# The first quarter of a feed-forward product, all of it in seven block products

## The chip, the cores and the metric

The kernel runs on one core of a Trainium2 chip. The core has five engines with an instruction stream each: TensorE (PE in the profile, its weight loads PEld), VectorE (DVE), ScalarE (ACT), GpSimd (POOL) and SyncE (SP), which here only issues DMAs. An engine works its stream in order, and engines wait for each other through semaphores. PE writes its results into PSUM, from where ACT and DVE take them. The metric is the time of one execution on the device in microseconds, the median of several runs.

## The reference

One layer of a streaming encoder on 512 rows of width 1024, in float32. Three branches of attention are gated, added up and projected; then comes the part that the change touches:

```python
h = h + merged @ w_out[l]
u2 = rmsnorm(h, g_ffn[l])
h = h + jnp.square(jax.nn.relu(u2 @ w_ff1[l])) @ w_ff2[l]
return rmsnorm(h, g_final)
```

`w_ff1` is 1024 x 4096, `w_ff2` 4096 x 1024.

## The kernel before, in words

**Products in three passes.** Operands are split into a high part in a rounded format (`hi`, a cast on ACT) and the remainder (`lo`, a subtraction on DVE). A product is then three matmuls: high by high, high by low, low by high. Every weight chunk of 128 x 1024 numbers (512 KB) is loaded into a buffer `raw`, cast, and subtracted. `raw`, `hi` and `lo` have three buffers each in the pool of weights, so a load waits until the chunk three before it has been split. In the last part every fourth `raw` has a buffer of its own in another pool.

**Seven products for eight.** The feed-forward part runs in four quarters of 1024 hidden columns. A quarter has two halves (`i` = 0, 1). Each half is `u2` (as two by two blocks) times a two by two block of `w_ff1`, computed by a scheme of seven block products (numbered 1 to 7) instead of eight. Products 1, 2 and 3 take a plain weight block ("11", "21", "22"); products 5, 6, 7 and 4 take the sums T1 to T4 of weight blocks. The sums are made in DRAM by DMAs on POOL's queue, early in the program: `sum_ops` lists them, and `next_sum` issues one behind the cast of each weight chunk, at line 131 if it adds to what is there and at 133 if it copies. On the side of the activations product 1, 2, 3 and 4 take a block of `u2`, products 5, 6 and 7 a difference of blocks (`u2s`, high and low part `u2sh`, `u2sl`); one block is replaced by the sum or difference `R7`. A block product is 24 matmuls of 128 x 128 by 256 columns into one PSUM bank; `first_evac` adds the seven up in SBUF, squares the positive part, and splits the result (`ch`, `cl`) for the second product.

**The first quarter is special.** Its second half (`first_product(0, 1)`) runs in block products. Its first half runs as four plain column tiles: tiles 0 and 1 in halves of 256 columns (`half`), between the transposes of the norm, and tiles 2 and 3 (`plain_tile`) as matmuls of 512 columns. So the differences of activations (`u2_sums`, line 1264) are made while the plain tiles run.

**What stands ahead.** The projection by `w_out` runs in two halves of 512 columns; the second one finishes row block by row block (`res_evac`). A finished block is squared and summed on ACT, one small power on POOL gives the norm's factor (`rr`, line 986), DVE scales the block (`un`, line 1190), PE transposes it (`u2_turn`, line 1214), ACT and DVE split it into `u2`, and ACT copies it to `b11` or `b12` (line 1217), from which the differences are made.

**What sets the order.** PE's stream is in the order of the code. The streams of the other engines are put in order by a scheduler from a model of its own; `tc.issue_after(x)` adds that an instruction comes behind `x`.

Of the kernel before, what the change touches and what calls it, by code (L numbers as in the profile page):

```python
# [32 lines left out]
def chunk_list():  # L33
# [24 lines left out]
    L += [("T", "w_ff1", P * j) for j in range(4)]  # L58
    for q in range(4):
        L += [(kind, q, i, b) for kind in "FB" for b in ("11", "21", "12", "22") for i in range(2) if kind == "B" or q or i]  # L60
# [4 lines left out]
def hybrid_block(ctx, tc, chunks, wst, memT, xN, gffn, gfin, wup, cst, out):  # L65
# [45 lines left out]
    tsum = {(n, q): dram.tile([2 if q else 1, P, 1024], F32, name=f"T{n}_{q}") for q in range(4) for n in (1, 2, 3, 4)}  # L111

    def sum_ops():
        for q in range(4):
            for n, src, add in ((1, "11", 0), (3, "12", 0), (1, "12", 1), (3, "22", 1), (2, 1, 0), (2, "22", 1), (4, 2, 0),
                                (4, "21", 1)):
                i = index["F", q, 0 if q else 1, src] if isinstance(src, str) else None
                yield tsum[n, q], tsum[src, q] if i is None else wst[i:i + (2 if q else 1)], add

    sums = sum_ops()  # L120
    chunk_n, cast_now, low_now, hold = [0], [None], [None], [None]

    def next_sum(after):
# [3 lines left out]
        op = next(sums, None) if n > 11 else None  # L127
        if op is not None:
            to, src, add_ = op
            if add_:  # L130
                d = nc.gpsimd.dma_start(to, src, accum_op=ALU.add, max_dma_last_dim=8192)
            else:
                d = nc.gpsimd.dma_start(to, src)
# [857 lines left out]
    with pool("outp") as op_:  # L991
# [28 lines left out]
        def gate_group(gate, wo, oh, ol, i, ready=None, last=None):  # L1020
# [65 lines left out]
            def merge(j):  # L1086
                th = X[j % 4 // 2][:, j % 2, :]
                nc.vector.scalar_tensor_tensor(th, th, 1.0, ys[j], op0=ALU.add, op1=ALU.mult)
                nc.gpsimd.tensor_tensor(acc[j], acc[j], th, op=ALU.add)
# [76 lines left out]
        gate_group("gate_gla", "w_gla_o", ogh, ogl, 1, last=(mh, ml))  # L1166
        hN = [h_tile(t, "h") for t in range(NT)]
# [12 lines left out]
        def res_evac(c):  # L1180
            def go(t, ps):
                cs = slice(512 * c, 512 * c + 512)
                nc.vector.tensor_tensor(hN[t][:, cs], hN[t][:, cs], ps, op=ALU.add)
                sumsq(unp.tile([P, 512], F32, tag="hsq", name=nm("hsq"), bufs=2), hN[t], t, c, c)
                if c == 1:
                    r = rms_tile(unp, t)
                    un[t] = unp.tile([P, D], F32, tag="un", name=nm("un"), bufs=2)
                    for g in range(2):
                        gs_ = slice(512 * g, 512 * g + 512)
                        nc.vector.scalar_tensor_tensor(un[t][:, gs_], hN[t][:, gs_], r, gf[:, gs_], op0=ALU.mult, op1=ALU.mult)  # L1190
            return go

        un = {}
# [14 lines left out]
        ws = [[t.rearrange("p (k c) -> p k c", k=KT) for t in own_w(("T", "w_ff1", P * j))] for j in range(2)]  # L1208

        def u2_turn(t):  # L1210
            for g in range(2):
# [4 lines left out]
                last = split(*(x[:, 2 * g + t // 2, :, sl] for x in u2), pt)  # L1216
# [3 lines left out]
        first = [mmt() for _ in ws]  # L1220

        def half(j, i, ks=range(KT)):
            sl = slice(256 * i, 256 * i + 256)
# [26 lines left out]
    with pool("ff") as yp:  # L1250
# [119 lines left out]
        def first_product(q, i):  # L1370
            for n in FIRST:
# [11 lines left out]
                if q == 0 and n == 2:  # L1383
                    u2_last()
# [222 lines left out]
```

## Time and profile before

| | us |
|---|---|
| median of 3 runs | 816.33 (816.24 to 818.31) |
| profiled execution, its own time | 815.97 |
| its span from the first to the last instruction | 814.2 |
| last merge on POOL ends | 447.5 |
| first and last transposes of the norm begin on PE | 481.10, 493.51 |
| second product begins on PE | 532.63 |

The page of the profile gives busy times by engine, the chain of waits that ended last, and groups of instructions. A row of instructions in order of time has the start in us from the begin of the span, the length in us, engine, line and operation, result and sources (buffer numbers left out), shape, and in brackets the idle time ahead with what ended it. Neighbours on PE overlap, so their distance is what one costs.

### The profile page before, as it was taken

How to read it: one execution, taken by the hardware profiler on the slowest of the kernel's cores; microseconds unless marked ns; L12 is line 12 of the kernel's file. 1: busy time of each engine (PE TensorE's matmuls, PEld its weight loads, DVE VectorE, ACT ScalarE, POOL GpSimd, SP SyncE). 2: the span in 40 equal slices, each digit the busy share in tenths (PEclk: the TensorE clock that was granted, in tenths of full speed). 3: DMA queues.
4: the chain of work that ended last, by engine and by line, in shares of the span. 5: the costliest groups of instructions: out<-in, count | busy, mean ns of one | idle time of the engine just before them, and what ended most of it. 6: DMA issues, size and time to landing. Idle time of an engine off the chain costs nothing.

```text
span 814.2 us, 12430 instructions
## 1 busy us (share of the span) xinstructions
PE 805.0 (99%) x4788; PEld 707.4 (87%) x4788; DVE 590.2 (72%) x913; ACT 438.7 (54%) x694; POOL 103.9 (13%) x127
## 2 busy tenths in 40 slices
PE   9999999999999999999999999999999999999996
PEld 7788888888888888999999889988998899889984
DVE  6857877546455587877567548896788778887896
ACT  7755655443344234444454536774676367637764
POOL 0000110011101212143143000011001100100011
PEclk9999999999999999999999999999999999999999
DMA  9433666688788867757755505878658855895543
GB/s 358 172 116 131 204 165 201 188 240 246 204 250 264 230 215 190 178 151 207 205 131 159 203 1 179 261 160 216 244 165 198 218 216 166 196 253 195 156 84 124
DMA packets 38604, 155.53 MB, mean 191 GB/s; under 512 B 4560, under 2 KB 5008, under 8 KB 36496
## 3 DMA queue, kind: packets, MB, share of 16 engines
q1 hardware_dynamic: 27424, 95.98, 32.8%
q0 software_dynamic: 9328, 54.01, 31.4%
q10 hardware_dynamic: 1792, 4.75, 1.6%
q8 instruction: 37, 0.61, 0.3%
q14 instruction: 23, 0.19, 0.1%
HBM read 152.58 MB, written 31.49 MB: 226 GB/s over the span
## 4 chain that ended last, share of the span: by engine, by line
PE 96%; DVE 1%; issue 1%; DMA 0%; ACT 0%; POOL 0%; POOLq 0%; DVEq 0%; ACTq 0%
PE mm L157 24%; PE mm L158 24%; PE mm L159 24%; PE a L157 5%; PE a L158 5%; PE a L159 5%; PE mm L380 1%; PE a L394 1%; PE a L624 1%; PE a L662 1%; PE a L661 1%; DVE h L1267 1%; PE a L900 1%; PE a L408 1%; DMA mem_s<-in_memT_dram 0%
## 5 line engine op out<-in xcount | busy, mean ns | idle before, releaser
L148 DVE TENSOR_TENSOR wlo<-raw,whi 128x1024 fp32r<-128x1024 f32 x67 | 86.4, 1293 | 58.9 <-ACT whi L147 58.7
L157 PE MATMUL mm<-uhi,whi 128*128 128x512 f32 (+1 forms) x352 | 125.9, 358 | 0.0
L159 PE MATMUL mm<-uhi,wlo 128*128 128x512 f32 (+1 forms) x352 | 123.7, 351 | 0.0
L158 PE MATMUL mm<-ulo,whi 128*128 128x512 f32 (+1 forms) x352 | 123.6, 351 | 0.0
L147 ACT CAST whi<-raw 128x1024 fp32r<-128x1024 f32 x67 | 70.4, 1051 | 92.9 <-PE mm L158 56.0
L1271 ACT CAST hi<-raw 128x1024 fp32r<-128x1024 f32 x65 | 68.2, 1049 | 49.7 <-PE mm L158 32.7
L1273 DVE TENSOR_TENSOR lo<-raw,hi 128x1024 fp32r<-128x1024 f32 x65 | 79.5, 1224 | 17.6 <-ACT hi L1271 17.6
L157 PEld LDWEIGHTS mm<-uhi,whi 128*128 128x128 f32 x352 | 66.7, 189 | 9.9 <-issue 1.5
L159 PEld LDWEIGHTS mm<-uhi,wlo 128*128 128x128 f32 x352 | 66.6, 189 | 9.1
L158 PEld LDWEIGHTS mm<-ulo,whi 128*128 128x128 f32 x352 | 66.7, 189 | 8.1
L1271 ACT CAST hi<-b 128x1024 fp32r<-128x1024 f32 x40 | 41.9, 1048 | 42.0 <-PE mm L159 25.6
L158 PE MATMUL mm<-u2l,hi 128*128 128x256 f32 x224 | 63.4, 283 | 0.0
L159 PE MATMUL mm<-u2h,lo 128*128 128x256 f32 x224 | 63.4, 283 | 0.0
L157 PE MATMUL mm<-u2h,hi 128*128 128x256 f32 x224 | 63.4, 283 | 0.0
L1457 POOL DMA_DIRECT2D b<-in_wst_dram x32 | 27.3, 853 | 271.3 <-DVE lo L1273 208.1
L1273 DVE TENSOR_TENSOR lo<-b,hi 128x1024 fp32r<-128x1024 f32 x40 | 48.9, 1224 | 14.1 <-ACT hi L1271 14.0
L158 PE MATMUL mm<-lo,ch 128*128 128x512 f32 x136 | 52.9, 389 | 0.0
L157 PE MATMUL mm<-hi,ch 128*128 128x512 f32 x136 | 52.9, 389 | 0.0
L159 PE MATMUL mm<-hi,cl 128*128 128x512 f32 x136 | 52.9, 389 | 0.0
L158 PE MATMUL mm<-u2sl,hi 128*128 128x256 f32 x168 | 47.5, 283 | 0.0
L157 PE MATMUL mm<-u2sh,hi 128*128 128x256 f32 x168 | 47.5, 283 | 0.0
L159 PE MATMUL mm<-u2sh,lo 128*128 128x256 f32 x168 | 47.5, 283 | 0.0
(414 smaller groups left out, 2093.2 us busy)
## 6 DMA issues: line engine op xcount, KB each, us to landing
raw<-in_wst_dram SPq DMA_DIRECT2D x114, 512.0 KB
b<-in_wst_dram POOLq DMA_DIRECT2D x32, 512.0 KB, 5.3
raw<-T SPq DMA_DIRECT2D x28, 512.0 KB
T<-in_wst_dram POOLq DMA_DIRECT2D x12, 1024.0 KB, 9.3
b<-in_wst_dram SPq DMA_DIRECT2D x16, 512.0 KB
wb<-in_wst_dram POOLq DMA_DIRECT2D x15, 512.0 KB, 5.3
wb<-in_wst_dram SPq DMA_DIRECT2D x8, 512.0 KB
nFb<-dF ACTq DMA_DIRECT2D x6, 512.0 KB
```

Of the source, the lines that this page charges most:

```text
L147: cast = nc.scalar.copy(hi, raw)
L148: low_now[0] = nc.vector.tensor_tensor(lo, raw, f(hi), op=ALU.subtract).ins
L157: nc.tensor.matmul(ps, lh, rh, start=start, stop=False, skip_group_check=on)
L158: nc.tensor.matmul(ps, lh, rl, start=False, stop=False, skip_group_check=on)
L159: nc.tensor.matmul(ps, ll, rh, start=False, stop=stop, skip_group_check=on)
L380: nc.tensor.matmul(kps[h], w[:, h * P:(h + 1) * P], x[:, k, :], start=k == p == 0, stop=k == KT - 1 and p == 2)
L394: nc.tensor.matmul(ps, x[:, k, sl], w[low][:, kk, :], start=k == low == 0 and x is mxh, stop=k == KT - 1 and low == 1)
L408: nc.tensor.transpose(pt[:, t * P:(t + 1) * P], xn[:, t, k * P:(k + 1) * P], ident)
L624: nc.tensor.matmul(ps[e], q[a, sl], k[a, :w], start=p == 0, stop=p == 2)
L1271: nc.scalar.copy(hi, raw)
L1273: nc.vector.tensor_tensor(lo, raw, f(hi), op=ALU.subtract)
L1457: nc.gpsimd.dma_start(to[i], wst[index["B", q, i, x]], accum_op=ALU.add)
```

## The change

The four plain tiles are gone; half 0 of the first quarter runs in block products too, with its own chunks of `w_ff1` (loads of "F" chunks instead of "T" chunks). The halves take turns: product 1 and 2 of half 0, then of half 1, then 5, 5, 6, 6, 3, 3, 7, 7, 4, 4. Each half has two PSUM banks, and some products are added up there: 6, 7 and 4 are accumulated onto 1, and 3 onto 5. For that the sign of product 6's difference is turned round. A product of this list runs its high-weight passes first and the low-weight ones last (`low_last`). The evacuations, casts, subtractions and loads of this quarter are written out in one list, and `in_order` keeps that order on DVE, ACT and SP. Eight more sums (a fifth group of T1 to T4, for half 0) are issued on POOL's queue two at a time behind the casts of `w_out` chunks, after the last merge. The load of the last norm's gains (`gl`) is put behind the loads of the last quarter's blocks.

POOL's stream between the last merge and the norm, before (`acc`: merges; `rr`: powers of the norm; waits in brackets are semaphores of the engines and of DMA landings):

```order
L1089 TENSOR_TENSOR acc6_1905<-acc6_1905,ct_630_4085 128x512 [waits DVE_49,Pool_49]
L1089 TENSOR_TENSOR acc7_1906<-acc7_1906,ct_630_4085 128x512 [waits DVE_49,Pool_49]
L1089 TENSOR_TENSOR acc4_1903<-acc4_1903,ct_629_4084 128x512 [waits DVE_49,Pool_49]
L1089 TENSOR_TENSOR acc5_1904<-acc5_1904,ct_629_4084 128x512 [waits DVE_49,Pool_49]
L986 TENSOR_TENSOR rr_706_4614<-ms_705_4613,mhalf_73 128x1 [waits DVE_49]
L986 TENSOR_TENSOR rr_710_4648<-ms_709_4647,mhalf_73 128x1 [waits DVE_49]
```

and after:

```order
L1089 TENSOR_TENSOR acc5_1908<-acc5_1908,ct_629_4088 128x512 [waits DVE_49,Pool_49]
L133 DMA T1_4_93<-in_wst_dram 16x8192 [waits DMASW7_49]
L133 DMA T3_4_95<-in_wst_dram 16x8192
L131 DMA T1_4_93<-in_wst_dram 64x2048 [waits DMASW7_49]
L131 DMA T3_4_95<-in_wst_dram 64x2048 [waits DMASW2_49,DMASW0_49]
L133 DMA T2_4_94<-T1_4_93 16x8192 [waits DMASW3_49,DMASW1_49,Activation_49]
L131 DMA T2_4_94<-in_wst_dram 64x2048 [waits DMASW3_49]
L133 DMA T4_4_96<-T2_4_94 16x8192 [waits DMASW4_49,Activation_49]
L131 DMA T4_4_96<-in_wst_dram 64x2048 [waits DMASW6_49,DMASW5_49]
L986 TENSOR_TENSOR rr_706_4626<-ms_705_4625,mhalf_73 128x1 [waits DVE_49]
L986 TENSOR_TENSOR rr_710_4660<-ms_709_4659,mhalf_73 128x1 [waits DVE_49]
```

Eight DMAs now stand ahead of the first power, six of which wait for the landing of an earlier one of the eight.

DVE's stream from the last differences on, before (`b`: differences of activations; `u2sl` their low parts; `lo` low parts of weights; `R`: the half-wide sums):

```order
L1264 TENSOR_TENSOR R70_4912<-b111_4415,b110_4414 128x512
L211 TENSOR_TENSOR u2sl_4915<-b121_4417,u2sh_4914 128x1024
L1264 TENSOR_TENSOR R71_4913<-b111_4415,b110_4414 128x512
L211 TENSOR_TENSOR u2sl_4915<-b120_4416,u2sh_4914 128x1024
L211 TENSOR_TENSOR u2sl_4915<-b110_4414,u2sh_4914 128x1024
L1273 TENSOR_TENSOR lo_754_5050<-raw_752_5047,hi_753_5049 128x1024
```

and after, from the second difference's low part on:

```order
L1357 TENSOR_TENSOR lo_750_4982<-raw_745_4892,hi_749_4981 128x1024
L1367 TENSOR_TENSOR u2sl_4877<-b110_4418,u2sh_4876 128x1024
L1283 TENSOR_TENSOR ev1_4865<-ev1_4865,mm_724_4714 128x512
L1357 TENSOR_TENSOR lo_753_5016<-raw_748_4950,hi_752_5015 128x1024
L1280 TENSOR_TENSOR R70_4874<-b111_4419,b110_4418 128x512
L1280 TENSOR_TENSOR R71_4875<-b111_4419,b110_4418 128x512
```

Between the differences stand now the low parts of the weights of products 5 and 6 and the additions of products 1 and 2.

ACT's stream after, where product 6 of half 1 gets its weights (`hi_755`; `raw_751` holds them):

```order
L1365 CAST u2sh_4876<-b110_4418 128x1024
L1353 CAST hi_752_5015<-raw_748_4950 128x1024
L1413 COPY od0_4866<-mm_723_4713 128x512
L1305 ACTIVATE ev1_4865<-ev1_4865 128x512
L1306 ACTIVATE ev1_4865<-ev1_4865 128x512
L1365 CAST u2h_4406<-R70_4874 128x512
L1365 CAST u2h_4406<-R71_4875 128x512
L1353 CAST hi_755_5053<-raw_751_4988 128x1024
```

The cast of these weights stands behind the casts of both `R`; before, the casts of `R` stood among the plain tiles' evacuations.

The diff, cut to its core:

```diff
-    L += [("T", "w_ff1", P * j) for j in range(4)]
...
-    tsum = {(n, q): dram.tile([2 if q else 1, P, 1024], F32, name=f"T{n}_{q}") for q in range(4) for n in (1, 2, 3, 4)}
+    tsum = {(n, q): dram.tile([2 if 0 < q < 4 else 1, P, 1024], F32, name=f"T{n}_{q}") for q in range(5) for n in (1, 2, 3, 4)}
...
+    sums, late_sums = islice(sum_ops(), 32), islice(sum_ops(), 32, None)
...
+        for to, src, add_ in islice(late_sums if late_on else sums, 1 + len(late_on)):
+            with tc.issue_after(merged[0]) if late_on else ExitStack():
+                if add_:
+                    d = nc.gpsimd.dma_start(to, src, accum_op=ALU.add, max_dma_last_dim=8192)
+                else:
+                    d = nc.gpsimd.dma_start(to, src)
...
-        ws = [[t.rearrange("p (k c) -> p k c", k=KT) for t in own_w(("T", "w_ff1", P * j))] for j in range(2)]
+        ws = [own_w(("F", 0, 0, b)) for b in ("11", "21")]
...
-                last = split(*(x[:, 2 * g + t // 2, :, sl] for x in u2), pt)
+                if g or t < 2:
+                    last = split(*(x[:, 2 * g + t // 2, :, sl] for x in u2), pt)
...
+            for low in range(1 + low_last):
+                for a in range(2):
+                    for k in range(4):
+                        if not low:
+                            mm(a, k, wh, uh, k == 0 if go is None else go and a == k == 0, False)
+                            mm(a, k, wh, ul, False, False)
+                        if low or not low_last:
+                            mm(a, k, wl, uh, False, k == 3 and (go is None or a == 1))
+                        yield
...
         u2_turn(2)
-        half(0, 0)
-        half(1, 0, range(4))
+        run(first_mms(1, ws[0], banks[0][0], True))
+        rest = first_mms(2, ws[1], banks[0][1], True)
+        run(islice(rest, 4))
         norm_end = u2_turn(3)
-        half(1, 0, range(4, KT))
-        half(0, 1)
-        half(1, 1)
+        run(rest)
...
+            for n, behind in ((1, added[3]), (2, scaled[3])):
+                get(n, 1)
+                high(n, 1)
+                with tc.issue_after(behind):
+                    low(n, 1)
+            get(5, 0)
+            get(5, 1)
+            mms(1, 1)
+            mms(2, 1)
+            with tc.issue_after(norm_end), in_order():
+                nc.scalar.copy(o11[0], flat[0][1])
+                sub(b_22, b_21, b_22)
+                high(5, 0)
+                add(o11[0], flat[0][0])
+                part(sums[0], b_22)
+                low(5, 0)
+                get(6, 0)
+                part(sums[0], b_22, True)
+                mms(5, 0)
+                relu2(o11[0])
+                sub(b_21, b_11, b_21)
+                sub(b_11, b_22, b_11)
+                high(5, 1)
+                nc.scalar.copy(o11[1], flat[1][1])
+                left_high(0, 0, o11[0])
+                part(sums[1], b_11)
+                low(5, 1)
+                get(6, 1)
+                mms(5, 1)
+                part(sums[1], b_11, True)
+                high(6, 0)
+                add(o11[1], flat[1][0])
+                low(6, 0)
+                get(3, 0)
+                mms(6, 0)
+                nc.scalar.copy(o22[0], flat[0][1])
+                relu2(o11[1])
+                for k in range(2):
+                    sub(R7[k], b_12[:, 512 * k:512 * k + 512], b_11[:, 512 * k:512 * k + 512], ALU.add)
+                    part(fours[k], R7[k])
+                high(6, 1)
+                for k in range(2):
+                    part(fours[k], R7[k], True)
+                low(6, 1)
+                get(3, 1)
+                mms(6, 1)
...
-        plain_evac(0, first[0])
-        plain_evac(1, first[1])
-        plain_tile(2)
-        u2_sums()
-        plain_tile(3)
-        load_blocks(0)
-        first_product(0, 1)
+        first_quarter()
         second_product(0)
```

`high` is the cast of a weight chunk, `low` its subtraction, `get` its load, `part` the high or low part of a difference, `mms` the 24 matmuls of one product; the rest of the list goes on in the same way through products 3, 7 and 4.

More of the change, by code (lines that the diff above doesn't have):

```diff
@@ L1 @@
-from contextlib import ExitStack
+from contextlib import ExitStack, contextmanager
 from functools import partial
@@ L126, in next_sum @@
         n = chunk_n[0]
[L127 to L133, printed above, removed]
+        if n <= 11:
+            return
+        for to, src, add_ in islice(late_sums if late_on else sums, 1 + len(late_on)):
[4 more added lines that the diff above has]
+                    d = nc.gpsimd.dma_start(to, src)
             tc.add_manual_dep(d.ins, after.name, mybir.DependencyInfo(mybir.DependencyClass.Sync, mybir.DependencyReason.DATA),
```

196 lines of the change are left out of this document (127 added, 69 removed).

## The prediction

> **What bounds the kernel now.** I read the page's busy shares and its chain first, then the instructions in order of time around the place of the change.
>
> ```profile
> PE 805.0 (99%) x4788; PEld 707.4 (87%) x4788; DVE 590.2 (72%) x913; ACT 438.7 (54%) x694; POOL 103.9 (13%) x127
> PE 96%; DVE 1%; issue 1%; DMA 0%; ACT 0%; POOL 0%; POOLq 0%; DVEq 0%; ACTq 0%
> ```
>
> TensorE (PE) carries 96% of the chain that ends last, so a product that is left out is worth its issue interval, as long as its operands come in time. The next rows (instructions on PE in order of time: start, length, line, operation) mark the stage.
>
> ```profile
> 481.10 1.03 PE L1214 MATMUL a<-cst_s,un 128*128 128x128 f32 x8
> ...
> 493.51 1.04 PE L1214 MATMUL a<-cst_s,un 128*128 128x128 f32 x8
> 494.30 0.36 PE L157 MATMUL mm<-u2h,f3h 128*128 128x256 f32 x1
> ...
> 501.57 0.40 PE L157 MATMUL mm<-u2h,whi 128*128 128x512 f32 x1
> ...
> 512.48 0.28 PE L157 MATMUL mm<-u2h,hi 128*128 128x256 f32 x1
> ...
> 532.63 0.40 PE L157 MATMUL a<-hi,ch 128*128 128x512 f32 x1
> ```
>
> 481.10 is the first transpose of the normed rows (row block 0), 493.51 the last (block 3). From 494.30 stand 60 matmuls of 256 columns (rest of tiles 0 and 1), from 501.57 48 of 512 (tiles 2 and 3), from 512.48 168 of 256 (the seven block products of half 1); at 532.63 the second product begins. That is 7.27/60 = 0.121, 10.91/48 = 0.227 and 20.15/168 = 0.120 us each. Lengths of 0.28 and 0.40 overlap; only the distances count. There is no hole in this stage to win back.
>
> **The change, part by part.** *Products on PE.* In the first half of the quarter four column tiles (96 matmuls of 256 and 48 of 512) give way to 168 of 256. Up to 494.30 nothing moves: 36 matmuls of the first products stand before the last transposes in both. After it come 12 + 12 x 24 = 300 matmuls of 256, at 0.120 us 36.0 us, where 38.33 (532.63 - 494.30) stood: **-2.36 us** if every operand is there. The 512-wide matmul costs 0.227, less than two halves (0.240), so leaving out an eighth of the block work saves only 6% of the stage.
>
> *First wait: the first block product with a summed operand.* Product 5 of half 0 needs a difference of activations that only the last transposes complete. Before, 18 us of plain tiles covered it; now 12 + 48 matmuls, until 494.30 + 60 x 0.120 = 501.5. The costs, from before's ScalarE (ACT) and VectorE (DVE) rows:
>
> ```profile
> 495.49 1.18 ACT L1217 COPY b<-a 128x512 f32<-128x512 f32 x2 [0.27 <-DVE u2l L211]
> 502.27 1.04 ACT L210 CAST u2sh<-b 128x1024 fp32r<-128x1024 f32 x1
> 507.01 1.05 ACT L1271 CAST hi<-raw 128x1024 fp32r<-128x1024 f32 x1 [0.77 <-PE mm L158]
> 508.60 0.62 ACT L210 CAST u2h<-R 128x512 fp32r<-128x512 f32 x1
> 516.39 0.58 ACT L1347 COPY ev<-mm 128x512 f32<-128x512 f32 x1
> ...
> 495.97 2.35 DVE L148 TENSOR_TENSOR wlo<-raw,whi 128x1024 fp32r<-128x1024 f32 x2
> 499.37 3.74 DVE L1264 TENSOR_TENSOR b<-b,b 128x1024 f32<-128x1024 f32 x3
> 503.76 1.22 DVE L211 TENSOR_TENSOR u2sl<-b,u2sh 128x1024 fp32r<-128x1024 f32 x1
> 518.43 0.69 DVE L1349 TENSOR_TENSOR ev<-ev,mm 128x512 f32<-128x512 f32 x1
> ```
>
> The fixed order puts on ACT, ahead of the copy of the last transposed block, the copy of product 2's bank, which waits for product 2: 494.30 + 12 x 0.120 + 0.28 = 496.0. Then ACT does copy 0.58, cast of weights 1.05, copy 0.59, each starting 0.09 before the one ahead ends (DVE likewise: 2.35 for two of 1.22): 498.05. DVE: difference 1.22, sum of products 1 and 2 0.69, low part of the weights 1.22, low part of the difference 1.22, less 3 x 0.09 = 502.1. The high part (ACT, 1.04) fits inside. PE's second matmul of product 5 wants the low part at 501.6: **+0.5 us**.
>
> *Second wait: product 6 of half 1.* DVE goes on without a pause: two differences, two low parts of weights and one of a difference at 1.22, an addition and two half-wide sums (R) at 0.69: 5 x 1.22 + 3 x 0.69 - 8 x 0.09 = 7.45, so the second R stands at 509.6. ACT casts it (0.62) and only then the weights (1.05 - 0.09): 511.2. PE wants them three products of 2.88 after product 5's begin at 501.5 + 0.5: 510.6. **+0.6 us.** The differences of the three b<-b,b rows (1.26 apart rather than 1.13) would add 0.3; if the pipelines overlap more, both waits fall to zero. Ends: 0 and 1.6 for both together; I take 1.1, from the rows themselves. Later products have 0.5 us or more: the tightest is the subtraction that frees product 7's bank for product 4 of half 1. Two splits of a transposed block (0.62 on ACT, 0.69 on DVE each) fall away; ACT and DVE have that time free before 496, so they are worth nothing.
>
> *Eight more sums on POOL's queue.* They stand now between the last merge and the four small powers (rr) of the norm. Each waits for the landing of the one it reads, and POOL's queue is in order, so the first rr cannot start before the eighth is issued.
>
> ```profile
> 443.63 3.85 POOL L1089 TENSOR_TENSOR acc<-acc,ct 128x512 f32<-128x512 f32 x2 [2.70 <-DVE ct L1088]
> 472.25 0.57 POOL L986 TENSOR_TENSOR rr<-ms,mhalf 128x1 f32<-128x1 f32 x1 [24.76 <-DVE ms L985]
> ...
> 472.85 1.41 DVE L1190 SCALAR_TENSOR_TENSOR un<-h,rr,gf 128x512 f32<-128x512 f32 x2 [0.68 <-POOL rr L986]
> ...
> T<-in_wst_dram POOLq DMA_DIRECT2D x1, 512.0 KB, 4.0
> T<-T POOLq DMA_DIRECT2D x1, 512.0 KB, 4.3
> T<-in_wst_dram POOLq DMA_DIRECT2D x1, 512.0 KB, 5.1
> wb<-in_wst_dram POOLq DMA_DIRECT2D x2, 512.0 KB, 8.0
> q0 software_dynamic: 80, 0.52, 29.6%
> ```
>
> The last numbers of the DMA rows are us to landing: a copy from the weights 4.0, from a sum 4.3, an adding one alone 5.1, and 8.0 as the middle of two issued together. One adding DMA held 29.6% of the engines for 10.7 us, 3.2 us of all sixteen. From the merge's end at 447.5: 4.0 + 5.1 + 4.3 + 5.1 + 4.3, 3.2 for the other adding DMA ahead of the second copy, and 0.85 for the last issue: 474.3. Before, rr starts at 472.25; the first transposes at 481.10 need it 1.3 earlier (472.25 to half of the un row), by 479.8. So 2 us of delay, and 5.5 us of room: **0** here, with the far end in the rivals. By the Trainium skill, "DMA: Bandwidth & Descriptors", section "Anatomy of one DMA — SWDGE (gpsimd) path", such a DMA takes about 2.0 us plus bytes over 436e3, 3.2 us here, so that the queue would be free near 467 (an estimate from that page); the trace's 4.0 to 5.1 are longer, and they decide.
>
> *The same sums against the weight loads.* They fall into these stretches (columns: PE, PEld, DVE, ACT, POOL busy, clock, share of the DMA engines, GB/s):
>
> ```profile
> 450.00:455.00 5.00, 5.00 (x23) 4.13 (x23) 2.14 (x2) 1.67 (x2) 0.00 (x0) 1.00 0.79 265
> 455.00:460.00 5.00, 5.00 (x23) 4.13 (x22) 2.45 (x2) 1.53 (x3) 0.00 (x0) 1.00 0.46 164
> 460.00:465.00 5.00, 5.00 (x23) 4.13 (x22) 4.24 (x7) 3.05 (x6) 0.00 (x0) 1.00 0.59 215
> 465.00:470.00 5.00, 5.00 (x24) 4.14 (x23) 1.03 (x4) 2.30 (x6) 0.00 (x0) 1.00 0.29 94
> 470.00:475.00 5.00, 5.00 (x24) 4.14 (x23) 2.32 (x4) 0.73 (x2) 0.57 (x1) 1.00 0.00 0
> ...
> 460.61 1.04 ACT L147 CAST whi<-raw 128x1024 fp32r<-128x1024 f32 x1
> ```
>
> The loads hold all engines for 10.6 us of these (the shares added, times five). The four adding sums put 12.7 us on top (4 x 3.2), the copies between nothing and as much again; with half of it 19 us, together some 30 us from 447.5, until 477. So loads and sums will both land later than alone. The last chunk of w_out was cast at 460.61; PE needs it at 481.10 - 72 x 0.227 + 18 x 0.227 = 468.8. About 6 us of cover: 0; without it, each us late is a us of PE.
>
> *On SP's queue* product 5's weights of half 1 come behind two loads for product 6. The second of those waits for a buffer that DVE frees near 494.3; half 1's product 5 is cast near 501.5, 7 us later, where an adding DMA of the same size lands in 5.1: 0. The load of the last norm's gains (gl) moves from 494 to late in the program: 0, it is read only at the end. The changed sign of product 6 costs the same instruction.
>
> **Sum:** -2.36 + 0.5 + 0.6 = -1.2 us (rounded). The profiled run took 815.97 (span 814.2 and 1.8 around it), so 814.8 in its terms. The median of the three runs is 0.36 above it; there I forecast **815.1 us**, 0.15% faster, within what a measurement of this kernel can tell from no change (about 0.3%, 2.45 us).
>
> **The rivals.** *Full gain.* Both waits vanish, because the pipelines of ACT and DVE overlap more than 0.09 us or PE arrives later at product 5. For it: 1.1 us is little against seventeen instructions in a row. Against it: DVE is already 4.9 of 5 us busy just there, without the change.
>
> ```profile
> 500.00:505.00 5.00, 5.00 (x30) 4.40 (x29) 4.90 (x6) 3.23 (x5) 0.00 (x0) 1.00 0.93 300
> ```
>
> It gives 816.33 - 2.36 = 814.0; beyond 0.3% only with a little luck.
>
> *POOL's queue holds the norm (slower).* It decides once the five landings of the chain take 6.3 us on average, (479.8 - 0.85 - 447.5)/5, instead of 4.6 (5.2 with the other adding DMA). Speaking for it: the row of 8.0 for two issued together, and the loads that share the engines. Against it: the loads leave the engines alone from 470. At 7.1, halfway from 6.3 to 8.0, rr starts at 483.8, the transposes at 485.1 rather than 481.1: +4.0, in all +2.8, 819.1. At 8.0 throughout: 488.3, +8.5, 823.7. The Trainium skill ("SBUF — State Buffer", the warning of "the DVE blocks DMA trap") says that VectorE can keep GpSimd from writing a DMA's descriptors, which would lengthen these issues further. No row here shows an issue held so, and DVE is less than half busy from 450 to 460.
>
> *Loads come late in the quarter.* Half 0 takes seven loads instead of four, three of them waiting for buffers that the crowded DVE frees. A load 2 us behind its cover, once, gives back what is won: 816.3 to 817.5.
>
> **How the numbers follow.** My forecast 0.46 (own range 814.3 to 816.0: both waits from zero nearly to their upper end); full gain 0.17; POOL's queue 0.27; late loads 0.10. Faster by over 0.3% takes more than the full gain, and a reading in its favour: 0.11, out of the full gain and the edge of mine. Slower by over 0.3%: POOL's queue from a landing of 7 us up, 0.20, and 0.02 of the loads, 0.22. The rest, 0.67, is within. The range, 813.8 to 819.1, leaves out the far end of POOL's case and a reading below the full gain, about 0.2 together.
>
> **What would show it.** In the changed trace: about 300 matmuls of 256 in place of 38.33 us of the old ones; a hole of about 0.5 us one matmul into product 5 of half 0, ended by DVE; one of about 0.6 us at the begin of product 6 of half 1, ended by ACT; the second product's begin near 531.4 instead of 532.6; the eighth sum issued near 474 and the first rr right behind it, with the transposes still at 481.1. I am wrong if rr starts after 480, if a cast in the quarter waits for a DMA, or if holes of PE appear outside this stage.

## The result, and the profile after

The changed kernel took 821.05 us (median of 6 runs, 819.95 to 821.74) where the kernel before took 816.27 in the runs beside it: 1.0054 times as long, with an interval of 1.0041 to 1.0067. A second group of six runs gave 821.18 us (819.46 to 825.78), 1.0063 (1.0043 to 1.0083). The forecast was 815.1 us, 813.8 to 819.1. It is slower by 0.5%, and lies above the forecast range.

In some executions the first matmuls go slowly, which makes up to 2.2 us in the traces here, so the account below is made on a second trace of the changed kernel (820.41 us, span 818.6), which has only some 0.25 us of that; the first trace (821.56 us, span 819.8) has 2.2 us. The chain that ended last, in the second trace:

```profile
PE 87%; DVE 5%; DMA 4%; ACT 2%; issue 2%; POOL 0%; POOLq 0%; ACTq 0%; DVEq 0%
```

Before it was 96% PE and no DMA. VectorE and DMAs now stand in the chain. Where, the rows of PE show (second trace, in order of time):

```profile
482.23 1.32 PE L1216 MATMUL a<-cst_s,un 128*128 128x128 f32 x8 [0.70 <-DVE un L1191]
...
495.83 1.29 PE L1216 MATMUL a<-cst_s,un 128*128 128x128 f32 x8 [0.21 <-DVE un L1191]
496.87 0.36 PE L1231 MATMUL mm<-u2h,f3h 128*128 128x256 f32 x1
...
504.78 0.39 PE L1231 MATMUL mm<-u2sl,hi 128*128 128x256 f32 x1 [0.36 <-DVE u2sl L1367]
...
514.05 0.38 PE L1231 MATMUL mm<-u2sh,hi 128*128 128x256 f32 x1 [0.49 <-ACT hi L1353]
...
534.30 0.40 PE L157 MATMUL a<-hi,ch 128*128 128x512 f32 x1
...
546.39 0.50 PE L158 MATMUL a<-lo,ch 128*128 128x512 f32 x1 [0.76 <-DVE lo L1289]
...
550.53 0.50 PE L158 MATMUL a<-lo,ch 128*128 128x512 f32 x1 [1.09 <-DVE lo L1289]
```

Against the rows of before: the first transposes come at 482.23 instead of 481.10, and PE waits for the scaled row block; the first matmul behind the last transposes comes at 496.87 instead of 494.30, 2.57 later, of which some 0.25 is the start: 2.3 us lost at the norm. From there to the second product it is 534.30 - 496.87 = 37.43 us instead of 38.33: 0.9 gained, with the two forecast holes in their places (504.78 and 514.05; a bracket counts from the modelled end of the matmul ahead, by the distances of the starts the holes cost 0.59 and 0.75). The second product begins 1.67 late. Its product 5 then waits twice for the low part of its weights, and the span ends 4.4 late (818.6 against 814.2): 2.7 lost behind the begin of the second product. So 0.2 + 2.3 - 0.9 + 2.7 = 4.3 of the 4.4.

The norm. POOL's rows from the last merge's end on (second trace), and the fourth power of before:

```profile
447.71 1.08 POOL L133 DMA_DIRECT2D T<-in_wst_dram  x2
454.91 0.85 POOL L131 DMA_DIRECT2D T<-in_wst_dram  x1 [6.12 <-DMA T<-in_wst_dram]
...
463.10 0.52 POOL L133 DMA_DIRECT2D T<-T  x1 [6.17 <-issue]
470.34 0.77 POOL L131 DMA_DIRECT2D T<-in_wst_dram  x1 [6.72 <-DMA T<-T]
475.95 0.52 POOL L133 DMA_DIRECT2D T<-T  x1 [4.84 <-DMA T<-in_wst_dram]
480.00 0.79 POOL L131 DMA_DIRECT2D T<-in_wst_dram  x1 [3.53 <-DMA T<-T]
480.54 0.85 POOL L986 TENSOR_TENSOR rr<-ms,mhalf 128x1 f32<-128x1 f32 x1
...
494.21 0.55 POOL L986 TENSOR_TENSOR rr<-ms,mhalf 128x1 f32<-128x1 f32 x1 [5.28 <-DVE ms L985]
```

```profile
491.62 0.55 POOL L986 TENSOR_TENSOR rr<-ms,mhalf 128x1 f32<-128x1 f32 x1 [7.74 <-DVE ms L985]
```

The first power has no bracket: its operand had long been there, it stood behind the eighth sum, issued at 480.00. The five landings in the chain took 6.5 us on average (480.00 - 447.71, by five). The first power is 8.3 us later than before, the fourth 2.6: from block to block some of the delay is made up, but not all of it.

Product 5. POOL's adding DMAs for the second product, ACT's casts of product 5's weights and SP's load of `b12` (first trace, where PE's two holes stand at 547.46 and 551.60); then POOL's and SP's rows of before:

```profile
528.88 0.90 POOL L1582 DMA_DIRECT2D b<-in_wst_dram  x1 [32.77 <-DMA b<-in_wst_dram]
530.17 0.86 POOL L1582 DMA_DIRECT2D b<-in_wst_dram  x1 [0.39 <-issue]
533.53 0.85 POOL L1582 DMA_DIRECT2D b<-in_wst_dram  x1 [2.51 <-DVE lo L1289]
534.67 0.85 POOL L1582 DMA_DIRECT2D b<-in_wst_dram  x1 [0.28 <-DVE lo L1289]
...
545.10 1.05 ACT L1287 CAST hi<-b 128x1024 fp32r<-128x1024 f32 x1 [4.39 <-DMA b<-in_wst_dram]
548.94 1.05 ACT L1287 CAST hi<-b 128x1024 fp32r<-128x1024 f32 x1 [1.75 <-DMA b<-in_wst_dram]
...
521.62 1.95 SPq L1447 DMA_DIRECT2D b<-in_wst_dram  x2
```

```profile
508.99 0.88 POOL L1457 DMA_DIRECT2D b<-in_wst_dram  x1 [16.81 <-ACT sq L1303]
511.93 0.85 POOL L1457 DMA_DIRECT2D b<-in_wst_dram  x1 [2.07 <-DMA b<-in_wst_dram]
529.55 0.85 POOL L1457 DMA_DIRECT2D b<-in_wst_dram  x1 [16.77 <-DMA raw<-in_wst_dram]
532.67 0.85 POOL L1457 DMA_DIRECT2D b<-in_wst_dram  x1 [2.26 <-DVE lo L1273]
...
505.07 3.13 SPq L1449 DMA_DIRECT2D b<-in_wst_dram  x4
```

Before, SP loaded both pairs of blocks from 505.07 on; POOL added to `b12` (for product 7) at 508.99 and 511.93, and much later, alone, to `b11` (for product 5). In the changed list the load of `b12` comes at 521.62. The additions for product 7 wait for it and are issued at 528.88 and 530.17, and those for product 5 stand directly behind them: four in one queue within 6 us. Product 5's weights are needed first and land last: the cast at 545.10 waits 4.39 us for them, 11.6 us after their DMA was issued at 533.53.

### The profile page after: what moved, and what is told of

The parts are those of the page before. It is cut to its first block, busy times and chain, and to the rows that moved or that the text cites. A ratio compares the mean times of both kernels' runs of the same rounds, so it can differ in the third digit from the quotient of the medians.

```text
span 819.8 us, 12500 instructions
## 1 busy us (share of the span) xinstructions
PE 807.6 (99%) x4812; PEld 709.1 (86%) x4812; DVE 591.8 (72%) x913; ACT 441.4 (54%) x699; POOL 109.3 (13%) x135
## 4 chain that ended last, share of the span: by engine, by line
PE 83%; DMA 6%; DVE 5%; issue 2%; ACT 2%; POOL 1%; POOLq 0%; SPq 0%; ACTq 0%; DVEq 0%
PE mm L157 16%; PE mm L159 16%; PE mm L158 16%; PE mm L1231 15%; PE a L158 4%; PE a L159 4%; PE a L157 4%; DMA b<-in_wst_dram 2%; PE mm L380 2%; DMA raw<-in_wst_dram 1%; PE a L394 1%; DMA T<-T 1%; DMA T<-in_wst_dram 1%; DVE lo L1357 1%; DVE lo L1289 1%
## 5 line engine op out<-in xcount | busy, mean ns | idle before, releaser
L148 DVE TENSOR_TENSOR wlo<-raw,whi 128x1024 fp32r<-128x1024 f32 x65 | 84.6, 1305 | 60.9 <-ACT whi L147 60.6
L147 ACT CAST whi<-raw 128x1024 fp32r<-128x1024 f32 x65 | 68.4, 1052 | 94.2 <-PE mm L158 54.8
L1287 ACT CAST hi<-raw 128x1024 fp32r<-128x1024 f32 x58 | 60.8, 1049 | 45.5 <-PE mm L1231 30.2
L1289 DVE TENSOR_TENSOR lo<-raw,hi 128x1024 fp32r<-128x1024 f32 x58 | 70.9, 1222 | 14.7 <-ACT hi L1287 14.7
L1231 PE MATMUL mm<-u2l,hi 128*128 128x256 f32 x240 | 66.1, 283 | 0.0
L1231 PE MATMUL mm<-u2h,hi 128*128 128x256 f32 x240 | 66.1, 283 | 0.0
L1231 PE MATMUL mm<-u2h,lo 128*128 128x256 f32 x240 | 61.1, 283 | 0.0
L1231 PE MATMUL mm<-u2sh,hi 128*128 128x256 f32 x192 | 52.7, 283 | 0.5 <-ACT hi L1353 0.5
L1231 PE MATMUL mm<-u2sl,hi 128*128 128x256 f32 x192 | 52.6, 283 | 0.4 <-DVE u2sl L1367 0.4
```

The source lines that it names most:

```text
L147: cast = nc.scalar.copy(hi, raw)
L148: low_now[0] = nc.vector.tensor_tensor(lo, raw, f(hi), op=ALU.subtract).ins
L1231: nc.tensor.matmul(ps[:, a, :], x[:, a, k, :], y[:, s, k, :], start=start, stop=stop, skip_group_check=go is not None)
L1287: nc.scalar.copy(hi, raw)
L1289: nc.vector.tensor_tensor(lo, raw, f(hi), op=ALU.subtract)
```

## The experiments

**The sums moved to an earlier place.** All forty sums in one stream, one behind each cast:

```diff
-    sums, late_sums = islice(sum_ops(), 32), islice(sum_ops(), 32, None)
+    sums = sum_ops()
...
-        for to, src, add_ in islice(late_sums if late_on else sums, 1 + len(late_on)):
-            with tc.issue_after(merged[0]) if late_on else ExitStack():
+        for to, src, add_ in islice(sums, 1):
+            with ExitStack():
```

> The changed kernel, but the eight new sums follow the other 32 in POOL's queue, one behind each cast of a weight chunk, so that none stands between the last merge and the norm. Theory (POOL's queue holds the norm): in the changed kernel the first rr starts at 481.9, 32 us behind the merges' end, and the stretch from the first transposes to the first matmul behind the last ones grows from 13.2 us before to 14.6; here the first rr follows its ms at once, that stretch is 13.2 again, and the time falls by 1.5 us, to about 819.5. Rival 1: the stretch grew because ACT and DVE work in another order; then it stays at 14.6 and the time at 821. Rival 2: the sums only move their hold, to the adding DMAs of the gates between 310 and 350; then PE has new holes there and the gain is lost.

Measured: 831.52 us, 1.0185 (1.0172 to 1.0199). The hold was only moved: the last sums stand among the adding DMAs of the gates (`wb`), and those wait in the same queue. POOL's and PE's rows:

```profile
354.50 0.52 POOL L133 DMA_DIRECT2D T<-T  x1 [10.06 <-issue]
...
359.77 1.17 POOL L1032 DMA_DIRECT2D wb<-in_wst_dram  x1
...
370.67 0.58 PE L157 MATMUL mm<-f0h,whi 128*128 128x256 f32 x1 [7.51 <-ACT whi L147]
```

The `wb` of 359.77 stands behind two sums, of which the first waited 10 us; the cast of it waits for its landing until 369.57, and PE idles 7.5 us for these weights. With the smaller holes from 334 to 383 that makes 12.1 us. So the second rival came true, and the total says nothing on the norm. The trace does: the first power (487.98) waits for its operand again, and from the first transposes to the first matmul behind the last ones it is 13.21 us (496.83 to 510.04), as long as before, where the second trace of the changed kernel has 14.64. That is what the theory said of this stretch.

**Product 5's additions first.** One dependency more, in `factor`:

```diff
-                nc.gpsimd.dma_start(to[i], wst[index["B", q, i, x]], accum_op=ALU.add)
+                with tc.issue_after(adds[0]) if n == 7 and q == 0 else ExitStack():
+                    d = nc.gpsimd.dma_start(to[i], wst[index["B", q, i, x]], accum_op=ALU.add).ins
+                if n == 5:
+                    adds[0] = d
```

> The changed kernel, but in the first quarter's second product the two adding DMAs for product 7 (onto b12) are issued on POOL behind the two for product 5 (onto b11). In the changed kernel those for product 5 are issued at 533.5 and 534.7 and the first lands 11 us later, in time for a cast at 545.1; PE waits 0.5, 1.1 and 0.3 us at product 5, and the drift against before grows there from 3.0 to 5.4 us. Theory (four adding DMAs in one queue go one after the other, some 4.5 us each, and the two for product 7 stand ahead): the holes at product 5 vanish, 2 us or a little more are won, about 819. Rival: the landing is late because all DMA engines are full with weight loads; then the adding DMAs for product 5 land as late as now, or product 7 waits in their place, and the time stays within 0.5 us of 821.

Measured: 818.41 us, 1.0021 (1.0010 to 1.0031), 2.6 less than the changed kernel. The additions are issued from 534.76 on, those of product 5 ahead:

```profile
534.76 0.90 POOL L1583 DMA_DIRECT2D b<-in_wst_dram  x1 [37.43 <-DMA raw<-in_wst_dram]
535.90 2.61 POOL L1583 DMA_DIRECT2D b<-in_wst_dram  x3 [0.24 <-DVE lo L1289]
```

PE has no hole at product 5 any more, and from the second product's begin to the end of the span it is 281.61 us, as before (281.57). The order on POOL's queue was the cause.

**Both holes of the quarter moved.** Differences and low parts ahead of copies and sums, and product 6's weights ahead of `R7`:

```diff
-                nc.scalar.copy(o11[0], flat[0][1])
                 sub(b_22, b_21, b_22)
                 high(5, 0)
-                add(o11[0], flat[0][0])
                 part(sums[0], b_22)
+                part(sums[0], b_22, True)
+                nc.scalar.copy(o11[0], flat[0][1])
                 low(5, 0)
+                add(o11[0], flat[0][0])
                 get(6, 0)
-                part(sums[0], b_22, True)
...
+                high(6, 1)
+                low(6, 1)
                 for k in range(2):
...
-                high(6, 1)
...
-                low(6, 1)
```

> The changed kernel with two places of its list in another order: the first difference's high and low part stand ahead of the copy of product 2's bank, the addition and the weights' low part; and the cast and low part of product 6's weights (half 1) ahead of the two sums R and their casts. Theory of the prediction (two waits of 0.5 and 0.6 us, measured as holes of 0.5 and 0.7): both vanish, product 3 of half 0 still gets R in time, and the stretch from the last transposes to the second product falls from 37.4 to 36.1 us; the time falls by 1.2 us, to 819.8. Rival: ACT and DVE are simply full, so that the holes go elsewhere in the quarter; the stretch stays above 37.

Measured: 822.93 us, 1.0079 (1.0065 to 1.0092), 1.9 more than the changed kernel instead of 1.2 less. The two holes are gone, and one of 0.76 us stands at product 3 instead, ended by a cast of ACT, whose copies and squares now come later:

```profile
520.51 0.39 PE L1231 MATMUL mm<-u2h,hi 128*128 128x256 f32 x1 [0.76 <-ACT hi L1353]
```

From the last transposes to the second product it is 37.4 us, as without the move, so the loss is not made there. This trace also shows the hold in its dearest form; why the chain took longer, no run shows. POOL's chain took longer (eighth sum issued 34.9 us after the first), and PE waited 3.29 us for the first transposes; the windows behind it have the granted clock in the column after POOL's:

```profile
484.94 0.44 PE L1216 MATMUL a<-cst_s,un 128*128 128x128 f32 x2 [3.29 <-DVE un L1191]
```

```profile
484.94:486.80 1.86, 1.85 (x9) 1.62 (x10) 1.20 (x2) 0.56 (x2) 0.00 (x0) 0.69 0.97 203
486.80:488.00 1.20, 1.20 (x4) 0.91 (x4) 0.34 (x2) 0.63 (x3) 0.55 (x1) 0.50 0.09 14
488.00:489.00 1.00, 1.00 (x3) 0.77 (x3) 1.00 (x2) 0.00 (x0) 0.00 (x0) 0.50 0.00 0
489.00:491.00 2.00, 2.00 (x10) 1.58 (x9) 1.70 (x4) 1.02 (x3) 0.00 (x0) 0.98 0.04 12
```

The clock falls to 0.50 and is back at 489. PE's delay against the kernel before grows from 3.84 us at the transposes to 5.77 six microseconds on: the wait costs 1.9 us on top of itself. The Trainium skill ("TensorE: Matmul & The Clock Gate", part 1) has the array at half its rate after an idle window of about 3.4 us, and back after as much of work. This trace agrees in size: the wait is 3.29 us, and the granted clock goes to 0.50 inside the first window and is back some 3.4 us after that (finer windows put the fall near 485.7).

**The kernel before plus the eight sums.** Nothing else of the change:

```diff
-    sums = sum_ops()
+    sums, late_sums = islice(sum_ops(), 32), islice(sum_ops(), 32, None)
...
+        for to, src, add_ in islice(late_sums if late_on else sums, 1 + len(late_on)):
+            with tc.issue_after(merged[0]) if late_on else ExitStack():
```

> The kernel before, and to it nothing but the eight more sums, two at a time behind the casts of w_out and after the last merge, as in the changed kernel; nobody reads them. Theory (POOL's queue holds the norm): the eighth is issued 32 to 35 us after the last merge, near 481 to 483, the first power right behind it, the first transposes at 484 to 485.5 instead of 481.10, and the rest of the program keeps that: 819 to 821.5 us, of which up to 2 us would be TensorE running slower after the wait. Rival (the loss of the changed kernel is made inside the quarter, by its many steps on VectorE and ScalarE and by its loads): these sums cost nothing here, 816.0 to 816.8 us. Second rival (the sums cost by taking the DMA engines from the loads of w_out): holes of TensorE before 475, none at the transposes.

Measured: 819.12 us, 1.0034 (1.0021 to 1.0046), against 816.53 beside it: 2.6 us. POOL's rows, and PE's:

```profile
478.72 0.78 POOL L132 DMA_DIRECT2D T<-in_wst_dram  x1 [3.63 <-DMA T<-T]
479.25 0.84 POOL L987 TENSOR_TENSOR rr<-ms,mhalf 128x1 f32<-128x1 f32 x1
...
493.87 0.55 POOL L987 TENSOR_TENSOR rr<-ms,mhalf 128x1 f32<-128x1 f32 x1 [6.22 <-DVE ms L986]
```

```profile
481.35 1.03 PE L1216 MATMUL a<-cst_s,un 128*128 128x128 f32 x8
...
495.48 1.29 PE L1216 MATMUL a<-cst_s,un 128*128 128x128 f32 x8 [1.14 <-DVE un L1192]
```

The hold alone costs this much, and neither rival holds. The chain was shorter than the theory said (31.0 us from the first issue to the eighth), and the first transposes are not late at all (481.35; this trace started 0.25 late). The last ones are, by 1.97 with the start in it, and the first matmul behind them comes at 496.52, 2.22 late: 2.0 without the start. A first power at 479.25 is in time for block 0 and too late for block 3, because VectorE, whose stream is in order, scales block 0 only then, and the additions, square sums and powers of the later blocks queue behind it.

**T4's two sums behind the norm.** The changed kernel with the last two of the eight issued after the fourth power:

```diff
+                    if t == NT - 1:
+                        for to, src, add_ in last_sums:
+                            with tc.issue_after(powered[0]):
+                                nc.gpsimd.dma_start(to, src, **(dict(accum_op=ALU.add, max_dma_last_dim=8192) if add_ else {}))
```

> The changed kernel, but the last two of the eight sums (the copy and the addition for T4) are issued behind the norm's fourth power, near 496, instead of ahead of the first one. T4 is read last, near 521. Theory (POOL's queue holds the norm): the sixth sum is issued near 471, the first power comes when its square sum is there (near 472.3), the transposes come at 481.1 plus what the start of the program differs by, and about 3.3 us go: 821.05 - 4.78 = 816.27 is the kernel before, the quarter gives 0.9, product 5 of the second product costs 2.4 to 2.6, so 3.2 are left for the hold: 817.8 us (817.2 to 818.5). Rival (the norm comes late because of the DMA traffic itself, or the loss lies elsewhere): 820.5 to 821.5 us.

Measured: 818.05 us (816.15 to 821.16), 1.0014 (1.0001 to 1.0027), 3.0 less than the changed kernel. POOL's rows, and PE's at product 5:

```profile
468.11 0.77 POOL L132 DMA_DIRECT2D T<-in_wst_dram  x1 [4.07 <-DMA T<-T]
473.77 0.57 POOL L987 TENSOR_TENSOR rr<-ms,mhalf 128x1 f32<-128x1 f32 x1 [4.90 <-DVE ms L986]
```

```profile
547.20 0.50 PE L159 MATMUL a<-lo,ch 128*128 128x512 f32 x1 [1.12 <-DVE lo L1294]
```

The first power waits for its square sum again, and PE loses nothing at the norm. Product 5's hole stays, as expected.

**Both causes taken away.** The two edits together:

> As the run before it, and besides the adding DMAs of product 5 (second product, first quarter) stand ahead of those of product 7 on POOL's queue. Theory: only the gain of the quarter is left, 0.9 us below the kernel before: 815.4 us (814.9 to 815.9), and no hole of TensorE at product 5. Rival (the two causes overlap, so that taking both away gives less than the sum of 3.2 and 2.6): 816.3 us or more.

Measured: 815.66 us (815.42 to 818.5), 0.9997 (0.9988 to 1.0006) of before's 816.53 in the same session. The median is 0.9 lower, as expected from the quarter, but the interval takes in no change. Against the run before it 2.4 us are gone. The two causes add up: 3.0 and 2.4 are the 5.4 between this run and the changed kernel.

**Two swaps in the quarter.**

```diff
                 high(5, 0)
-                add(o11[0], flat[0][0])
                 part(sums[0], b_22)
                 low(5, 0)
                 get(6, 0)
                 part(sums[0], b_22, True)
+                add(o11[0], flat[0][0])
                 mms(5, 0)
+                high(5, 1)
                 relu2(o11[0])
...
-                high(5, 1)
...
+                high(6, 1)
                 for k in range(2):
...
-                high(6, 1)
```

> As the run before it, with two swaps in the written list: the low parts of product 5's weights and difference ahead of the sum of products 1 and 2 (and the next cast ahead of its square), and the cast of product 6's weights ahead of the half-wide sums R7. Theory (each of the two holes in the quarter is made by the place of one instruction): both go, 1.1 us less than the run before it, 814.3 us (813.9 to 814.8). Rival (ScalarE and VectorE have no room there, as when more was moved ahead and a hole of 0.76 us came at product 3): one hole comes back further on, 0.0 to 0.6 us less.

Measured: 815.24 us (814.91 to 815.89), 0.9982 (0.9973 to 0.9991): faster than both kernels, though by less than 0.3%; all eleven runs lie below the lowest of the 27 of before beside them (816.17). PE's rows:

```profile
513.15 0.62 PE L1236 MATMUL mm<-u2sh,lo 128*128 128x256 f32 x3 [0.50 <-DVE lo L1362]
...
531.49 0.40 PE L158 MATMUL a<-hi,ch 128*128 128x512 f32 x1
```

The second product begins at 531.49 instead of 532.63. Against the run before it 0.4 us are gone, which is the rival's number: of 1.1 us of holes one of 0.50 came back, at the low part of product 6's weights.

**A third swap**, `low(6, 1)` also ahead of `R7`:

> As the run with two swaps (815.24 us), with a third: the low part of product 6's weights (half 1) also ahead of the half-wide sums R7 on VectorE. There a hole of 0.50 us was left at TensorE, ended by just that low part. Theory: the hole goes, 0.4 to 0.6 us less, 814.7 us (814.4 to 815.0). Rival: the work pushed back (the low parts of R7, then the next casts) makes the next hole, 0 to 0.2 us less.

Measured: 816.11 us (815.14 to 817.13), 0.9994 (0.9985 to 1.0002). The hole went to product 3, and nothing was gained, even less than the rival said: from the last transposes to the second product its trace has 37.06 us, the run with two swaps 36.92.

```profile
514.43 0.39 PE L1236 MATMUL mm<-u2h,hi 128*128 128x256 f32 x1 [0.59 <-ACT hi L1358]
```

**The same eight DMAs, all of them copies.**

```diff
-                if add_:
+                if add_ and not late_on:
```

> The kernel before with the eight more DMAs, as in the run with the sums added to it (819.12 us), but the four adding ones copy instead (nobody reads the result). The same number of bytes comes from the weights, in the same order, with the same waits. Theory A (adding is what makes the landings long): the eighth is issued 5 us or more earlier than 478.72, so near 473, the last transposes stand within 0.5 us of 493.8, 816.3 to 817.0 us. Theory B (the weight loads that share the DMA engines, and the queue's own handling of one DMA behind another): the eighth is issued within 2 us of 478.7, 818.0 to 819.5 us.

Measured: 816.51 us (816.25 to 819.03), 1.0006 (0.9998 to 1.0015): no loss.

```profile
476.61 0.49 POOL L134 DMA_DIRECT2D T<-in_wst_dram  x1 [4.21 <-DMA T<-T]
477.11 0.58 POOL L987 TENSOR_TENSOR rr<-ms,mhalf 128x1 f32<-128x1 f32 x1
```

The chain is 28.7 us long instead of 31.0, so most of it comes with plain copies too. What adding costs of it is not settled by one trace each: the five traces with adding sums in this place range from 31.0 to 34.9. Neither theory is met cleanly: the time is that of A, the issue of the eighth nearer to B. What it does give is the edge: a first power at 477.11 costs nothing, one at 479.25 costs 2 us and more (both traces start some 0.25 late).

**Ten idle matmuls at the start**, the kernel before otherwise:

```diff
-        for _ in range(9):
+        for _ in range(10):
```

> The kernel before with ten instead of nine idle matmuls ahead of the first product, so that TensorE has almost no gap (0.47 us now) before the first real matmul. Some runs of most kernels are 1.5 to 2 us longer, and in the traces of such runs the first matmuls stand 0.213 us apart until 10.7 us in, rather than 0.12. Theory (the gap sometimes throws TensorE back to its slow pace): no run above 817 us, median 816.2. Rival (the pace depends on something that began before): a third of the runs is again near 818.

Measured: 816.31 us, all eleven runs between 815.97 and 816.76, while 7 of the 29 runs of before beside them were at 817.9 to 818.3. The runs came out as the theory has it, but not by its reason: the gap is 0.66 us here, wider than before, and the matmuls go fast at once. The eleven runs with two swaps, behind nine idle matmuls, were as even (814.91 to 815.89), so that this stays a hint. Nor does the gap sort the traces: behind 0.47, 0.82 (the sums alone) and 0.85 us (both holes moved) the first matmuls go fast, behind 0.52 and 0.73 us (first trace of the changed kernel, product 5's additions first) slowly.

```profile
5.65 0.74 PE L380 MATMUL mm<-mxh,hi 128*128 128x256 f32 x4 [0.66 <-ACT hi L274]
```

**The changed kernel again** gave the second trace shown above, as the median of the second group.

> The changed kernel once more, for a second trace. Its first trace began with the slow pace of the first matmuls, 2.2 us. Theory (that is not of the change; the hold and product 5 are): a trace with the quick start shows the transposes late by 3 us or more instead, since POOL's queue then has less time from the last merge on while its own chain takes as long (31 to 35 us), and product 5 late by 1.7 to 2.4 us; runs from 818.5 to 822. Rival (the slow start belongs to the changed kernel): every trace of it starts slow.

The slow start is not of the changed kernel: this trace has some 0.25 us of it. The norm is late by 2.3 us rather than by 3 or more, and product 5 costs 2.7 rather than up to 2.4.

**The kernel before again**, beside the first three of these runs:

> The kernel before once more, for its spread and a second profile of its start. In its profile the first matmuls of the memory keys ran 0.12 us apart from the first on, in the changed kernel's profile 0.21 us apart until 10.7 us, which put it back by 2.2 us. Theory (when the clock opens at the start differs from run to run): the runs of before fall into two groups some 2 us apart, 816.2 and 818.3, whatever the kernel. Rival: the start is a property of each kernel; then before's runs stay at 816.2 but for single ones and its profile shows 0.12 from the first matmul again.

Measured: 816.27 us (816.12 to 817.93), 0.9998 of the kernel before beside it. One run of these eleven, and four of the twenty beside them, lie above 817. In the trace the first four matmuls take 1.02 us from 5.70 instead of 0.58, and the transposes come 0.8 late. So the pace at the start is not fixed for a kernel, as the theory has it; no trace of before here has the full 2 us, so that its longest runs come from the start is not shown.

## Why the prediction was wrong

*The terms of the quarter held.* Forecast was -2.36 + 0.5 + 0.6 = -1.26 between the last transposes and the second product (at 0.120 each the first term is -2.33); measured -0.9 (37.43 against 38.33), with both holes in the places named, the first ended by DVE, the second by ACT, at 0.59 and 0.75. The 300 matmuls at 0.120 and the additions of rows on DVE and ACT were good to 0.4 us. The full gain was not reached by any of the three other orders tried: each closed one hole or two and opened another (0.76, 0.50 and 0.59 us).

*The step that failed is "Eight more sums on POOL's queue: 0".* Two sizes in it were wrong. First the chain: 26.9 us were forecast from the merge's end to the first power, and in the second trace it took 32.8 (447.71 to 480.54). By its issues, the copies that start the two pairs took 7.2 each instead of 4.0 and 4.3, the addition to T2 5.6 instead of 5.1; the two additions side by side (8.2 instead of 8.3) and the last copy (4.05 instead of 4.3) came as priced. The prices were single DMAs of the early program; the additions of 5.1 at 105.39 and 119.62 ran at a share of the DMA engines of 0.74 and 0.72, their own traffic in it. Here the loads run beside the sums. The stretch of the second copy, before and in the second trace (the share is the last but one column):

```profile
463.00:470.00 7.00, 7.00 (x33) 5.79 (x32) 3.02 (x8) 3.29 (x9) 0.00 (x0) 1.00 0.43 147
```

```profile
463.00:470.00 7.00, 7.00 (x32) 5.82 (x31) 3.77 (x8) 3.22 (x6) 0.52 (x1) 1.00 0.87 307
```

The prediction said so itself in its next paragraph ("loads and sums will both land later than alone", together until 477), and did not carry it back into its chain. But the two additions side by side came as priced at a share of 0.95, so the share alone does not explain it: how much of the excess is the loads' and how much is the queue's own, no run separates.

Then the room: 5.5 us were reckoned from the first transposes alone. The runs put the edge between a first power at 477.11 (no loss) and at 479.25 (2.0 us behind the last transposes), where the prediction had 479.8. The four powers are a chain of their own through VectorE, and its end counts.

*A term was missing.* Of POOL's queue the prediction counted only the eight sums. It moved SP's loads past each other for product 5's `w_ff1` weights, but not the load of `b12`, which now comes some 14 to 16 us later and takes the additions of the second product with it: 1.7 to 2.7 us in the five traces that have it, and 2.4 to 2.6 us less when their order is put right. That lies outside the stage, where the prediction's last sentence looked for trouble, and on the very queue it had in hand.

*The rivals.* "POOL's queue holds the norm" came true in its mechanism. That its price of 819.1 is also what the sums alone gave (819.12) is luck: the price has the gain of the quarter in it and landings of 7.1 us, the run has neither. By the same reckoning the first power of the second trace, at 480.54 instead of 479.8, costs 0.7 us at most; 2.3 were measured, because the room was taken at the first block. Its turning point of 6.3 us was a little high: the average was 6.3 and 6.5 in the two traces of the changed kernel, but 6.2 with the sums alone, which lost as well, and 5.7 with copies, which did not. The argument against it, that the loads leave the engines alone from 470, did not help, since the chain was late by then. "Loads come late in the quarter" did not occur there. The trap that the Trainium skill warns of ("SBUF — State Buffer", the warning in "SBUF: two separate sides", VectorE keeping GpSimd from writing descriptors) is not borne out: in the run with copies alone two copies between sums took 4.70 us each, from 461.26 with VectorE busy for 2.84 us of it and from 471.91 with 0.21. With adding sums in the chain no run tests it.

*Two of the three signs named* showed it: the first power after 480 (480.54), and holes of PE outside the stage (546.39 and 550.53). The third, a cast in the quarter that waits for a DMA, did not come; the casts that wait so stand in the second product.

## What to carry to other kernels

A DMA put into an engine's queue is priced by what stands behind it until the queue is free again, and a chain of DMAs that wait for each other's landing by the landings of that stretch, beside the loads that run there, not by single DMAs from elsewhere in the program. When a list of loads is written in another order, follow each load to the last instruction that waits for it on any queue, into the next stage: whoever is needed first must also be issued first. And where a delayed result opens a chain of blocks, the room is measured at the last block, not at the first.

## What was not expected of the hardware

- A wait of TensorE of 3.3 us at the transposes cost 1.9 us more, at a granted clock of 0.50 until 489; a wait of 7.51 us (sums at the earlier place) was followed by a clock of 0.50 too, from 372 to 374. Behind the waits of 0.70 us (second trace) and 1.14 us (sums alone) the eight transposes themselves took 0.25 to 0.3 us longer, and nothing more.
- The first matmuls of the program stand 0.213 us apart in some runs until 10.7 us, at a granted clock that is recorded as 1.00 all the while. Why is open. The first trace of the changed kernel:

```profile
5.73 1.22 PE L380 MATMUL mm<-mxh,hi 128*128 128x256 f32 x4 [0.52 <-ACT hi L274]
6.75 1.05 PE L380 MATMUL mm<-mxl,hi 128*128 128x256 f32 x4
```

- DMAs of 512 KB between places in DRAM that wait for each other took 4.05 to 8.8 us each from issue to issue (two side by side up to 9.2); with copies in place of the four adding ones the chain of five took 28.7 us, with them 31.0 to 34.9.
